# One attention tile per tick, two waves for the combination, and drains by name, in a hybrid decoder step

## The chip, the cores and the metric

The kernel runs on one core of a Trainium2 chip. The metric is the time of one execution on the device, in microseconds. The time before is the median of three runs. The engines are called by their short names: PE (TensorE, matrix products and transposes), DVE (VectorE), ACT (ScalarE), POOL (GpSimd) and SP (SyncE, which here issues every DMA, in the order of the program).

## The reference

One layer of a decoder trunk on a prompt of 1024 rows and a sample of 8 x 4 rows, D = 1024, all in float32:

```
h = RMSNorm(x);  [q|k|v|z|xBC|dt] = h @ w_in
attention: 12 heads of 64, RMS norm of q and k, ALiBi; three groups of 4 heads, (window, dilation) =
    (128,1), (512,4), (2048,16); query t reads t, t-d, ... t-window
    o_g = softmax(q k / 8 + bias) v;  alpha = softmax over g of lse_g;  att = concat(o_g * alpha_g)
SSD: causal conv (width 4) + SiLU on xBC; chunked scan, 16 heads of 64, state 128; D skip;
    * SiLU(z); RMSNorm
x = x + concat(att, ssd) @ w_out
u = causal conv (width 3) of RMSNorm(x) @ w_up;  x = x + (SiLU(gate) * up) @ w_down
```

The prompt and the sample are two batches with the same weights. The sample's attention also reads caches of keys and values, its SSD a state. New keys, values, states and convolution tails are outputs too.

## The kernel before

**Products.** Every projection is done three times, in a high and a low part: `hi x hi`, `hi x lo` and `lo x hi` (lines 1079 to 1081). Weights arrive by DMA (`w_load`), ACT makes the high part and DVE the low part (`w_split`, line 1069); three raw tiles and two high tiles take turns. A *chunk* is 128 output features for all 1056 rows, in three *units* of 352 columns; a unit of the xBC and z projections is 24 matmuls into one of three PSUM tiles `p_mm`, which DVE evicts (lines 1247 and 1561, scaled by the row factors `rb`).

**Stages.** First q, k and v of the three head groups (to about 332 us), with attention of groups 0 and 1 beside it. Then 12 xBC chunks, 8 z chunks, the out projection in two halves (attention, then SSD), and the feed-forward part.

**The side queues.** All other work is written as generators, held in named queues of a `Side` object. After each unit the program calls `tick`, which takes one step of each active generator; a generator that has just given PE work yields True, and is continued by `pre`, right after the next unit's matmuls and before that unit's eviction. So a generator's steps stand in the instruction streams between the units, and each engine runs its own stream in order. `add(name, gens, width, gap)` holds at most `width` active generators and opens one each `gap` ticks. `drain(names)` calls `pre` and `tick` with no unit between until the named queues are empty; `tick` steps all queues there.

**Around the change.** `att_gen` does one tile of 128 queries of one group: load of `qt` from the DRAM scratch `qscr`, transposes (line 663), scores into the one `p_sa` tile (682), bias and maximum by DVE (689), `Exp` by ACT (695), transposes (704), products with v (720), copies out (736). For group 2 a unit loads its rows by two strided DMAs (line 656), and takes a tick each for load, transposes, scores, exponential, transposes and products; its copies come with the next `pre`. `samp_gen` does the sample's attention of a group with POOL products and DVE sums, one cache tile `kt` a tick; `samp_comb` combines the groups for the sample (line 897 are its products). `comb_gen` waits for both and combines the prompt's groups: it makes the factors, transposes them (932), writes them to `fscr` and reads them back broadcast into `F` tiles, multiplies six tiles `c` = 0 to 5 by them (954, on POOL for even c and DVE for odd c) and stores them to `attscr`. Then the SSD opens (`ssd_gen`, first PE work at line 1298), and z chunk 4 may start only when the first SSD group is through and its gate is applied. `samp_ssd` is the sample's SSD; its first products are line 1475. `at_first` loads the combined tiles back and splits them into A0h/A0l and A1h/A1l, the moving tensors of the out projection.

**Memory.** SBUF tiles lie at addresses written out in `PLACES`; tiles whose lifetimes don't meet may share bytes, and a first write waits for the last reader of what lay there.

Of the kernel before, what the change touches and what calls it, by code (L numbers as in the profile page):

```python
# [10 lines left out]
F32 = mybir.dt.float32  # L11
# [8 lines left out]
S = 1024  # L20
# [96 lines left out]
def raw_ap(base, offset, dims):  # L117
# [28 lines left out]
    "P": ([128, 1024], F32, 2, 1, 2), "PT": ([128, 1024], F32, 1, 1, 2),  # L146
    "bias2": ([128, 4, 128], F32, 1, 3, 3.3), "qt2": ([128, 768], F32, 3, 3, 3.3), "qT2": ([128, 512], F32, 2, 3, 3.3),
    "P2": ([128, 512], F32, 2, 3, 3.3), "PT2": ([128, 512], F32, 1, 3, 3.3),
    "cs": ([128, 8, 3, 8], F32, 1, 3.5, 3.5), "mn": ([128, 8, 4], F32, 1, 3.5, 3.5), "ce": ([128, 8, 3, 4], F32, 1, 3.5, 3.5),
    "cwt": ([128, 8, 3, 4], F32, 1, 3.5, 3.5), "fT": ([12, S], F32, 1, 3.5, 3.5), "F": ([128, S], F32, 3, 3.5, 3.5),  # L150

    "sq_q": ([128, 1024], F32, 1, 1, 3), "so": ([128, 1024], F32, 1, 1, 3.3), "kt": ([128, 1024], F32, 3, 1, 3),
    "pr": ([128, 768], F32, 2, 1, 2), "bl": ([128, 144], F32, 1, 1, 3), "sc": ([128, 144], F32, 1, 1, 3),
    "ml0": ([128, 32], F32, 1, 1, 3.3), "ml1": ([128, 32], F32, 1, 1, 3.3), "ml2": ([128, 32], F32, 1, 1, 3.3),
    "snm": ([128, 128], F32, 1, 2, 3.3), "b16": ([128, 128], F32, 1, 2, 3.3), "bsel": ([128, 8], F32, 1, 2, 3.3),
    "smt": ([16, 136], F32, 1, 2, 3.3), "ats": ([128, 6, NS], F32, 1, 2, 3.3),

# [33 lines left out]
PLACES = {  # L191
    "ident": (77376,), "ones": (77984,), "neghalf": (77888,), "rb": (224992,), "rtok": (214272,), "ss": (155328,),
    "rr": (214848,), "cw": (112288,), "triu": (76832,), "par": (55744,), "pk": (69792,), "dt": (5248,),
    "acum": (70880,), "dend": (75488,), "cdec": (76064,), "acs": (56256,), "dtw": (70816,), "e128": (76000,),
    "cdecs": (76576,), "dsk": (65664,), "dsk2": (55680,), "rT": (214336,), "xsp": (33728,), "dtr": (32576,),
    "qg": (218432,), "xh": (163584,), "xl": (121536,), "xt": (56320, 20160, 35808, 24256), "jk": (16064,),
    "sx": (28352, 14016), "xr": (1152, 3200, 39904, 30400), "cst_in": (214848,), "cst_g": (33152,),
    "wqkl": (155392, 113344), "wqkh": (5824, 220480), "wvl": (201728, 41952), "wvh": (46304, 197376),
    "sb": (103072, 53280, 101024, 92832, 90784), "sq": (110240, 50656), "sm": (55424, 35776, 55392, 55648),
    "AU0": (78496,), "AU1": (20288,), "AU2": (43712,), "ac": (14144, 1152, 65696, 71392),  # L200
    "stt": (5024, 55456, 5152, 5088, 55328), "bias": (86688,), "qt": (94880, 97952, 38880, 1280),
# [5 lines left out]
    "ats": (8928,), "dt_x": (24064,), "dt_e": (20864,), "dt_s": (26688,), "dt_q": (21440,), "dt_p": (20288,),  # L207
    "na": (14016,), "acT": (4352,), "acTT": (24640, 22016), "wl": (10048, 117440, 159488), "wh": (155392, 113344),
    "XSa": (197376,), "XSb": (18368,), "zsm": (68768,), "ssq": (39360,), "BCa": (78496,), "BCb": (95392,),
    "BCs": (220256,), "xss": (60544,), "stc": (220768,), "ncv": (214848,), "st_in": (5824,), "ci0": (39360,),  # L210
    "ci1": (86688,), "acc": (91040, 107680), "zt": (52032, 220768, 14144, 43584), "Ab": (5824, 47808, 56320),
    "M": (61568, 103584), "xdt": (216160, 218208, 71392), "xdw": (35264, 73440), "cbm": (3200, 67744, 4224),
    "hn": (65696, 1152), "ho": (37312,), "sAb": (2176,), "sxdt": (61568,), "sxdw": (86816,), "scbm": (111904,),
# [5 lines left out]
    "facc": (219776, 197376, 30752), "nf": (9664, 39264, 9856, 9760, 39168, 213984, 9952, 9568), "tst": (214912,),  # L219
}  # L220
# [34 lines left out]
class Side:  # L255
# [7 lines left out]

    def add(self, name, gens, width=2, gap=1):
        ent = self.q.setdefault(name, [[], [], width, gap, 0])
        ent[0] += list(gens)
# [12 lines left out]

    def tick(self):  # L280
        waits = [g for _, g in self.early]
        for ent in list(self.q.values()):
            waiting, active, width, gap, left = ent
            ent[4] = max(left - 1, 0)
            if len(active) < width and waiting and not ent[4]:
                active.append(waiting.pop(0))
                ent[4] = gap
            for g in list(active):
                if not any(g is w for w in waits):
                    self.step(ent, g)  # L290
        self.q = {n: e for n, e in self.q.items() if e[0] or e[1]}

    def drain(self, names=None):
        while set(self.q) & set(names or self.q):
            self.pre()
            self.tick()


def body(tc, A):
# [338 lines left out]
    def bias_load(g, at):  # L638
# [3 lines left out]
        bias_t[g] = b  # L642

    def att_gen(g, i, at):
        qt = R("qt" + at)
        full = qscr[g].rearrange("t w c -> t (w c)")
        if g == 0:
            SP.dma_start(qt, full[i * 128:(i + 1) * 128, :])
            first = i == 0
        elif g == 1:  # L650
            r, blk = divmod(i, 2)
            SP.dma_start(qt, full[blk * 512 + r:(blk + 1) * 512:4, :])
            first = blk == 0
        else:
            for e in range(2):
                SP.dma_start(qt[e * 64:(e + 1) * 64], full[2 * i + e:S:16, :])
            first = True
# [85 lines left out]
    def att_chain(g, at):  # L743

        gens = [att_gen(g, i, at) for i in range(8)]
        return gens
# [9 lines left out]
    def samp_gen(g):  # L756
# [38 lines left out]
        for w, c in order:  # L795
# [40 lines left out]
            else:  # L836
# [5 lines left out]
                if c:  # L842
                    V.tensor_tensor(o, o, kt, op=ALU.add)
        done.add(("samp", g))
        yield
        SP.dma_start(oscr[g], o)
        yield

    def samp_comb():
# [7 lines left out]
        bsel = R("bsel")  # L857
        SP.dma_start(bsel, A["bsel"])
        yield
        ps = p_st()  # L860
# [26 lines left out]
        for g in range(3):  # L887
            o = R("so")
            SP.dma_start(o, oscr[g])
            yield  # L890
            V.tensor_tensor(o.rearrange("p (e d) -> p e d", d=64), o.rearrange("p (e d) -> p e d", d=64),
                            nm[:, 32 + g * 16:48 + g * 16, None].to_broadcast([128, 16, 64]), op=ALU.mult)
            yield
            for j in range(2):
                for t in range(4):
                    c = (2 * g + j) * NS + t * 8
                    T.matmul(ps[:, c:c + 8], lhsT=o[:, t * 256 + j * 128:t * 256 + (j + 1) * 128], rhs=bsel,
                             start=True, stop=True)
# [7 lines left out]
    def comb_gen():  # L906
# [40 lines left out]

        f_load(0)
        f_load(1)
        f_load(2)  # L950
        yield
        yield
        for c in range(6):
            (V if c % 2 else G).tensor_tensor(acs_[c], acs_[c], Fs.pop(c), op=ALU.mult)
            if c % 2:
                yield
                for x in (c - 1, c):
                    SP.dma_start(attscr[x, :, 0:S], acs_[x])
            if c < 3:
                f_load(c + 3)  # L960
        yield
# [181 lines left out]
    def group_end(g):  # L1143

        AUg[g] = R(f"AU{g}")
        if g < 2:
            bias_load(g, "")
            side.add("att", att_chain(g, ""), 4, 2)
        else:
            bias_load(2, "2")  # L1150
            side.add("att", att_chain(2, "2"), 4, 2)
        side.add("kvout", [kv_out(g)], 1)
# [429 lines left out]
    def at_low(c):  # L1582
        h, (raw, lo) = AT[c]
        (V if c % 3 else G).tensor_tensor(lo, raw, f32(h), op=ALU.subtract)

    def at_first():
        at_load(0)
        yield
        yield
# [8 lines left out]
    for f in range(8):  # L1598
        z_chunk(12 + f, f)
    at_load(1)  # L1600
    run_post(99)
# [299 lines left out]
```

## Time and profile before

| | |
|---|---|
| median of three runs | 1681.27 us (1681.21 to 1682.15) |
| profiled execution | 1682.31 us, of which the trace spans 1680.5 |
| PE busy | 1611.2 us |
| DVE, ACT, POOL busy | 1022.3, 618.5, 367.3 us |
| DMA | 159.9 MB, mean 95 GB/s |
| mean granted clock of PE | 0.985 |

The times of the trace count from the start of its span. A row of the timeline names an instruction's start, its duration, engine, line, operation, output and inputs, and in brackets how long the engine had been idle before it and what ended that. A granted clock of 1.00 is 2.4 GHz, one of 0.50 is 1.2 GHz.

### The profile page before, as it was taken

What the parts mean: (1) busy time and instruction counts of PE and PEld (TensorE: products, weight loads), DVE (VectorE), ACT (ScalarE), POOL (GpSimd) and SP (SyncE); (2) the same over time, 40 slices, a digit from 0 to 9 for tenths busy, and PEclk for the clock granted to TensorE, in tenths of its full rate; (3) what the DMA queues carried; (4) which work ended last, traced back from release to release, by engine and by line L of the source; (5) the groups of instructions that cost most, each with busy time, mean ns of one, the idle gap of its engine ahead of it and who ended that gap; (6) DMA issues with size and microseconds to landing.
All of it is one profiled execution on the core that took longest, in us unless ns stands there. A gap on an engine that the chain in (4) does not pass through costs nothing.

```text
span 1680.5 us, 26456 instructions
## 1 busy us (share of the span) xinstructions
PE 1611.2 (96%) x10543; PEld 1520.8 (90%) x10543; DVE 1022.3 (61%) x1714; ACT 618.5 (37%) x1144; POOL 367.3 (22%) x400
## 2 busy tenths in 40 slices
PE   7999989979979999799999999999999999999998
PEld 5787866879978888699999999999999999999998
DVE  5657648546557686874554665555655556555565
ACT  6534534436526876531223322131221312213121
POOL 3555345420023566420111100000000000000000
PEclk9999999989989999899999999999999999999999
DMA  7562365673392221574113102111021110211102
GB/s 216 160 185 66 115 214 165 208 177 113 86 248 98 67 95 57 170 210 119 43 43 101 52 26 68 48 39 52 26 67 49 38 52 26 65 51 38 52 1 105
DMA packets 174475, 159.91 MB, mean 95 GB/s; under 512 B 18851, under 2 KB 151355, under 8 KB 174352
## 3 DMA queue, kind: packets, MB, share of 16 engines
q1 hardware_dynamic: 174351, 158.22, 31.4%
q8 instruction: 83, 1.36, 0.3%
q14 instruction: 41, 0.33, 0.1%
HBM read 127.37 MB, written 34.42 MB: 96 GB/s over the span
## 4 chain that ended last, share of the span: by engine, by line
PE 72%; DVE 3%; DMA 2%; ACT 2%; issue 2%; POOL 1%; SPq 0%; DVEq 0%; POOLq 0%; ACTq 0%
PE p_up L1079 10%; PE p_up L1080 10%; PE p_up L1081 10%; PE p_mm L1079 6%; PE p_mm L1081 6%; PE p_mm L1080 6%; PE p_dn L1835 5%; PE p_dn L1836 5%; PE p_dn L1837 5%; DMA F<-fscr 1%; PE p_sa L1337 1%; DMA qt<-qscr 1%; PE p_sa L1330 1%; PE p_sa L1335 0%; POOL Ab L1322 0%
## 5 line engine op out<-in xcount | busy, mean ns | idle before, releaser
L1079 PE MATMUL p_up<-x2h,wh 128*128 128x352 f32 x1032 | 334.7, 324 | 0.0
L1080 PE MATMUL p_up<-x2l,wh 128*128 128x352 f32 x1032 | 333.4, 323 | 0.0
L1081 PE MATMUL p_up<-x2h,wl 128*128 128x352 f32 x1032 | 332.2, 322 | 0.0
L1745 DVE TENSOR_TENSOR fci<-p_up,rb 128x352 f32<-128x352 f32 x129 | 66.2, 513 | 238.1 <-PE p_up L1081 236.5
L1080 PEld LDWEIGHTS p_up<-x2l,wh 128*128 128x128 f32 x1032 | 194.3, 188 | 0.0
L1079 PEld LDWEIGHTS p_up<-x2h,wh 128*128 128x128 f32 x1032 | 193.8, 188 | 0.2
L1081 PEld LDWEIGHTS p_up<-x2h,wl 128*128 128x128 f32 x1032 | 193.8, 188 | 0.0
L1839 DVE TENSOR_TENSOR yacc<-yacc,p_dn 128x352 f32<-128x352 f32 x264 | 133.6, 519 | 75.2 <-PE p_dn L1837 75.2
L1835 PE MATMUL p_dn<-gp,dh 128*128 128x352 f32 x528 | 172.2, 326 | 0.0
L1836 PE MATMUL p_dn<-gp,dh 128*128 128x352 f32 x528 | 171.0, 324 | 0.0
L1837 PE MATMUL p_dn<-gp,dl 128*128 128x352 f32 x528 | 170.8, 323 | 0.0
L1081 PE MATMUL p_mm<-xh,wl 128*128 128x352 f32 x480 | 157.0, 327 | 10.0 <-DVE wl L1069 10.0
L1079 PE MATMUL p_mm<-xh,wh 128*128 128x352 f32 x480 | 162.6, 339 | 0.0
L1080 PE MATMUL p_mm<-xl,wh 128*128 128x352 f32 x480 | 156.3, 326 | 0.0
L1071 ACT CAST wh<-wl 128x512 fp32r<-128x512 f32 (+1 forms) x160 | 92.2, 606 | 112.1 <-PE p_up L1080 76.5
L1069 DVE TENSOR_TENSOR wl<-wl,wh 128x512 fp32r<-128x512 f32 (+1 forms) x160 | 126.0, 787 | 3.8 <-ACT wh L1071 3.7
L1763 DVE SCALAR_TENSOR_TENSOR facc<-fci,cw,facc 128x1072 f32<-128x1072 f32 x88 | 116.8, 1327 | 2.4 <-ACT facc L1755 2.4
L1782 ACT CAST gp<-facc 128x1024 fp32r<-128x1024 f32 (+1 forms) x44 | 25.7, 631 | 216.1 <-DVE facc L1778 216.1
L1081 PEld LDWEIGHTS p_mm<-xh,wl 128*128 128x128 f32 x480 | 91.6, 191 | 10.8 <-DVE wl L1069 10.8
L1835 PEld LDWEIGHTS p_dn<-gp,dh 128*128 128x128 f32 x528 | 99.2, 188 | 0.7 <-DVE yacc L1839 0.7
L1836 PEld LDWEIGHTS p_dn<-gp,dh 128*128 128x128 f32 x528 | 99.4, 188 | 0.0
L1837 PEld LDWEIGHTS p_dn<-gp,dl 128*128 128x128 f32 x528 | 99.1, 188 | 0.0
(390 smaller groups left out, 3436.9 us busy)
## 6 DMA issues: line engine op xcount, KB each, us to landing
wl<-in_w_up_dram SPq DMA_DIRECT2D x44, 512.0 KB
dl<-in_w_down_dram SPq DMA_DIRECT2D x22, 512.0 KB
kt<-in_cache_kv_dram SPq DMA_DIRECT2D x20, 512.0 KB
wl<-in_w_in_dram SPq DMA_DIRECT2D x20, 512.0 KB
Ab<-acscr SPq DMA_DIRECT2D x16, 512.0 KB
wqkl<-in_w_in_dram SPq DMA_DIRECT2D x24, 256.0 KB
qscr<-sb SPq DMA_DIRECT2D x24, 256.0 KB
qt<-qscr SPq DMA_DIRECT2D x16, 384.0 KB
```

What stands on the lines that cost most here:

```text
L1069: V.tensor_tensor(lo[:, c], raw[:, c], f32(hi[:, c]), op=ALU.subtract)
L1071: AC.copy(hi[:, c], raw[:, c])
L1079: T.matmul(ps[:, :CH], lhsT=hi[:, c], rhs=mh[:, c0:c0 + CH], start=k == 0, stop=False)
L1080: T.matmul(ps[:, :CH], lhsT=hi[:, c], rhs=ml_[:, c0:c0 + CH], start=False, stop=False)
L1081: T.matmul(ps[:, :CH], lhsT=lo[:, c], rhs=mh[:, c0:c0 + CH], start=False, stop=k == len(moving) - 1)
L1745: V.tensor_tensor(ci[:, 2 + c0:2 + c0 + w], ps[:, :w], r2t[:, c0:c0 + w], op=ALU.mult)
L1763: V.scalar_tensor_tensor(acc[:, :L], ci[:, i:i + L], cw_f[:, i, fu:fu + 1], acc[:, :L], op0=ALU.mult, op1=ALU.add)
L1782: AC.copy(hi, src)
L1835: T.matmul(ps[:, :CH], lhsT=hi[:, mc], rhs=GP[:, s2, c], start=x == 0, stop=False)
L1836: T.matmul(ps[:, :CH], lhsT=hi[:, mc], rhs=GP[:, s2 + 1, c], start=False, stop=False)
L1837: T.matmul(ps[:, :CH], lhsT=lo[:, mc], rhs=GP[:, s2, c], start=False, stop=x == len(fs) - 1)
L1839: V.tensor_tensor(yacc[:, m, c], yacc[:, m, c], ps[:, :CH], op=ALU.add)
```

## The change

- `add` has a `lead`: the number of ticks before the first generator opens. Group 2's attention now has width 8, gap 1 and lead 3 in place of width 4 and gap 2; its two first tiles are loaded in `group_end`, ahead of the bias; its `qt2` ring has six tiles in place of three.
- `samp_comb` loads the two stored results of the sample's groups at its start, into tiles of their own, keeps the third in SBUF without storing it, and multiplies the three without a tick for each load.
- `comb_gen` loads c = 0 to 2, waits three ticks, multiplies all three, then loads c = 3 to 5 and stores 0 to 2, waits three ticks, multiplies, and stores 3 to 5 two ticks later.
- `drain(names)` steps only the named queues, all queues each eighth time.
- `at_first` issues the loads of both halves of the combined tiles; the low part of c = 3 is made by DVE, not POOL.
- All addresses in `PLACES` are new, by a table not shown here. Of the tiles that the text speaks of, each 4224 bytes a partition, the four z buffers `zt` move from 52032, 220768, 14144, 43584 to 64384, 29408, 68608, 25184, and the three `A1h` from 14144, 52032, 43584 to 24928, 29152, 98176.

```diff
-    "bias2": ([128, 4, 128], F32, 1, 3, 3.3), "qt2": ([128, 768], F32, 3, 3, 3.3), "qT2": ([128, 512], F32, 2, 3, 3.3),
+    "bias2": ([128, 4, 128], F32, 1, 3, 3.3), "qt2": ([128, 768], F32, 6, 3, 3.3), "qT2": ([128, 512], F32, 2, 3, 3.3),
...
-    def add(self, name, gens, width=2, gap=1):
-        ent = self.q.setdefault(name, [[], [], width, gap, 0])
+    def add(self, name, gens, width=2, gap=1, lead=0):
+        ent = self.q.setdefault(name, [[], [], width, gap, lead])
...
-    def tick(self):
+    def tick(self, names=None):
         waits = [g for _, g in self.early]
-        for ent in list(self.q.values()):
+        for name, ent in list(self.q.items()):
+            if names is not None and name not in names:
+                continue
...
     def drain(self, names=None):
+        n = 0
         while set(self.q) & set(names or self.q):
+            n += 1
             self.pre()
-            self.tick()
+            self.tick(names if n % 8 else None)
...
+    def qt_strided(qt, i):
+        full = qscr[2].rearrange("t w c -> t (w c)")
+        for e in range(2):
+            SP.dma_start(qt[e * 64:(e + 1) * 64], full[2 * i + e:S:16, :])
+
+    ready = {}
+
     def att_gen(g, i, at):
-        qt = R("qt" + at)
+        qt = ready.pop((g, i)) if (g, i) in ready else R("qt" + at)
...
         else:
-            for e in range(2):
-                SP.dma_start(qt[e * 64:(e + 1) * 64], full[2 * i + e:S:16, :])
+            if i > 1:
+                qt_strided(qt, i)
             first = True
...
+        os_ = [R("sq_q"), R("so2"), last_o[0]]
+        for g in range(2):
+            SP.dma_start(os_[g], oscr[g])
...
         for g in range(3):
-            o = R("so")
-            SP.dma_start(o, oscr[g])
-            yield
+            o = os_[g]
...
-        f_load(0)
-        f_load(1)
-        f_load(2)
-        yield
-        yield
-        for c in range(6):
-            (V if c % 2 else G).tensor_tensor(acs_[c], acs_[c], Fs.pop(c), op=ALU.mult)
-            if c % 2:
+        for c in range(3):
+            f_load(c)
+        for half in range(2):
+            for _ in range(3):
                 yield
-                for x in (c - 1, c):
-                    SP.dma_start(attscr[x, :, 0:S], acs_[x])
-            if c < 3:
-                f_load(c + 3)
+            for c in range(3 * half, 3 * half + 3):
+                (V if c % 2 else G).tensor_tensor(acs_[c], acs_[c], Fs.pop(c), op=ALU.mult)
+            yield
+            if half:
+                yield
+            for c in range(3 * half, 3 * half + 3):
+                if c < 3:
+                    f_load(c + 3)
+                SP.dma_start(attscr[c, :, 0:S], acs_[c])
...
+            for i in range(2):
+                ready[2, i] = R("qt2")
+                qt_strided(ready[2, i], i)
             bias_load(2, "2")
-            side.add("att", att_chain(2, "2"), 4, 2)
+            side.add("att", att_chain(2, "2"), 8, 1, 3)
...
-        (V if c % 3 else G).tensor_tensor(lo, raw, f32(h), op=ALU.subtract)
+        (V if c else G).tensor_tensor(lo, raw, f32(h), op=ALU.subtract)
 
     def at_first():
         at_load(0)
+        at_load(1)
...
-    at_load(1)
     run_post(99)
     side.drain({"ssd", "yg", "conv_out", "at", "kvout"})
```

## Rows read from the trace of the kernel before

**Rows 1.** The page, part 1: PE's busy time, share and instructions.

```profile
PE 1611.2 (96%) x10543; PEld 1520.8 (90%) x10543; DVE 1022.3 (61%) x1714; ACT 618.5 (37%) x1144; POOL 367.3 (22%) x400
```

**Rows 2.** Waits of PE over the span: total us, times, longest.

```profile
PE p_st L663 <- DMA qt<-qscr: 14.4, 2, 9.7
PE p_mm L1081 <- DVE wl L1069: 10.0, 2, 6.0
...
PE p_st L1475 <- issue: 4.8, 1, 4.8
...
PE p_mm L1080 <- POOL A1l L1584: 2.0, 1, 2.0
```

**Rows 3.** Windows: busy us (instructions) of each engine, granted clock, DMA share, GB/s.

```profile
332.00:350.00 18.00, 8.26 (x52) 8.00 (x51) 2.25 (x4) 1.50 (x3) 2.34 (x3) 0.79 0.98 235
350.00:446.00 96.00, 95.87 (x676) 90.14 (x674) 58.41 (x149) 57.32 (x134) 13.32 (x24) 0.99 0.45 123
446.00:476.00 30.00, 30.00 (x190) 29.78 (x191) 18.92 (x35) 14.23 (x20) 2.65 (x7) 1.00 0.49 121
476.00:500.00 24.00, 13.98 (x75) 13.24 (x74) 11.15 (x11) 2.47 (x5) 5.78 (x6) 0.85 1.01 268
...
692.00:712.00 20.00, 15.20 (x94) 12.66 (x92) 17.77 (x12) 10.54 (x13) 11.58 (x5) 0.69 0.18 50
...
712.00:897.00 185.00, 185.00 (x1267) 178.64 (x1265) 104.31 (x171) 54.84 (x101) 31.77 (x17) 1.00 0.35 102
...
350.00:352.00 2.00, 2.00 (x9) 2.00 (x8) 0.00 (x0) 0.59 (x1) 1.31 (x2) 0.50 0.56 156
```

**Rows 4.** Timeline of SP's queue near 335 us; last, the chain's DMA row.

```profile
332.94 0.44 SPq L1230 DMA_DIRECT2D rb<-rscr  x1
...
335.23 0.66 SPq L759 DMA_DIRECT2D sq_q<-qs  x1
...
337.18 1.32 SPq L656 DMA_DIRECT2D qt<-qscr  x2
...
337.91 11.44 DMA qt<-qscr
```

**Rows 5.** Timelines of DVE and POOL, 338 to 358 us.

```profile
338.35 0.53 DVE L1247 TENSOR_TENSOR ci<-p_mm,rb 128x352 f32<-128x352 f32 x1 [9.74 <-DMA rb<-rscr]
...
347.91 2.34 POOL L832 TENSOR_TENSOR kt<-kt,sq_q 128x1024 f32<-128x1024 f32 x1 [15.63 <-DMA kt<-in_cache_kv_dram]
...
356.01 1.21 DVE L834 TENSOR_REDUCE sc<-kt 128x16 f32<-128x1024 f32 x1
357.13 0.28 DVE L689 CUSTOM_DVE_ANT_0 P<-p_sa,bias 128x128 f32<-128x128 f32 x1
```

**Rows 6.** Timeline of PE: the combination's transposes, and the SSD's first work.

```profile
465.27 1.03 PE L932 MATMUL p_st<-ident,ce 128*12 128x128 f32 x8
...
506.79 0.60 PE L1298 MATMUL p_st<-ident,XSa 128*128 128x128 f32 x4
```

**Rows 7.** Timelines of DVE and POOL at the combination's products.

```profile
480.12 1.23 DVE L954 TENSOR_TENSOR ac<-ac,F 128x1024 f32<-128x1024 f32 x1 [2.34 <-DMA ac<-attraw]
...
490.04 1.23 DVE L954 TENSOR_TENSOR ac<-ac,F 128x1024 f32<-128x1024 f32 x1 [6.81 <-DMA F<-fscr]
...
485.27 2.35 POOL L954 TENSOR_TENSOR ac<-ac,F 128x1024 f32<-128x1024 f32 x1 [2.19 <-DMA F<-fscr]
```

**Rows 8.** Timeline of ACT: first and last instruction for one SSD unit.

```profile
538.19 2.44 ACT L1314 ACTIVATE M<-Ab,acum 128x128 f32<-128x128 f32 x8
...
542.91 1.04 ACT L1316 ACTIVATE Ab<-Ab 128x1024 f32<-128x1024 f32 x1
```

**Rows 9.** Timelines of DVE and ACT at the end of the z chunks.

```profile
692.33 2.96 DVE L1584 TENSOR_TENSOR A0l<-A0l,A0h 128x1056 fp32r<-128x1056 f32 x1 [0.45 <-ACT A0h L1580]
...
696.70 1.25 DVE L1584 TENSOR_TENSOR A0l<-A0l,A0h 128x1056 fp32r<-128x1056 f32 x1
...
701.21 6.38 DVE L1584 TENSOR_TENSOR A1l<-A1l,A1h 128x1056 fp32r<-128x1056 f32 x2
...
700.24 1.08 ACT L1580 CAST A1h<-A1l 128x1056 fp32r<-128x1056 f32 x1 [0.76 <-POOL ssq L1549]
```

More of the change, by code (lines that the diff above doesn't have):

```diff
@@ L150 @@
     "cwt": ([128, 8, 3, 4], F32, 1, 3.5, 3.5), "fT": ([12, S], F32, 1, 3.5, 3.5), "F": ([128, S], F32, 3, 3.5, 3.5),
-    "sq_q": ([128, 1024], F32, 1, 1, 3), "so": ([128, 1024], F32, 1, 1, 3.3), "kt": ([128, 1024], F32, 3, 1, 3),
+    "sq_q": ([128, 1024], F32, 1, 1, 3.3), "so": ([128, 1024], F32, 1, 1, 3.3), "so2": ([128, 1024], F32, 1, 3, 3.3), "kt": ([128, 1024], F32, 3, 1, 3),
     "pr": ([128, 768], F32, 2, 1, 2), "bl": ([128, 144], F32, 1, 1, 3), "sc": ([128, 144], F32, 1, 1, 3),
@@ L155 @@
     "snm": ([128, 128], F32, 1, 2, 3.3), "b16": ([128, 128], F32, 1, 2, 3.3), "bsel": ([128, 8], F32, 1, 2, 3.3),
-    "smt": ([16, 136], F32, 1, 2, 3.3), "ats": ([128, 6, NS], F32, 1, 2, 3.3),
+    "smt": ([16, 136], F32, 1, 3, 3.3), "ats": ([128, 6, NS], F32, 1, 3, 3.3),
     "dt_x": ([128, 9, 16], F32, 1, 1, 1), "dt_e": ([128, 9, 16], F32, 1, 1, 1), "dt_s": ([128, 9, 16], F32, 1, 1, 1),
@@ L191 @@
 PLACES = {
[L192 to L201, printed above, removed]
[5 rows of a table removed]
@@ L207 @@
[L207 to L211, printed above, removed]
@@ L212 @@
-    "M": (61568, 103584), "xdt": (216160, 218208, 71392), "xdw": (35264, 73440), "cbm": (3200, 67744, 4224),
-    "hn": (65696, 1152), "ho": (37312,), "sAb": (2176,), "sxdt": (61568,), "sxdw": (86816,), "scbm": (111904,),
[5 rows of a table removed]
-    "facc": (219776, 197376, 30752), "nf": (9664, 39264, 9856, 9760, 39168, 213984, 9952, 9568), "tst": (214912,),
+    "ident": (19584,), "ones": (20096,), "neghalf": (20608,), "rb": (203776,), "rtok": (20704,), "ss": (20768,),
+    "rr": (19296,), "cw": (54624,), "triu": (220288,), "par": (159104,), "pk": (222336,), "dt": (223360,),
@@ new lines @@
+    "acum": (220800,), "dend": (221312,), "cdec": (221824,), "acs": (223936,), "dtw": (224000,), "e128": (224064,),
+    "cdecs": (224128,), "dsk": (54560,), "dsk2": (18752,), "rT": (55680,), "xsp": (41568,), "dtr": (159616,),
+    "qg": (127360,), "xh": (72832,), "xl": (169984,), "xt": (37472, 33376, 64384, 11904), "jk": (5760,),
+    "sx": (1152, 45664), "xr": (16000, 3712, 9856, 47712), "cst_in": (15168,), "cst_g": (3200,),
+    "wqkl": (203776, 56192), "wqkh": (25184, 211968), "wvl": (123008, 20832), "wvh": (68480, 224384),
@@ new lines @@
+    "sb": (43616, 110720, 134528, 49760, 106624), "sq": (120960, 51808), "sm": (160192, 160224, 160256, 160288),
+    "AU0": (139648,), "AU1": (11392,), "AU2": (3200,), "ac": (64384, 123264, 25184, 36608),
+    "stt": (53856, 53920, 53984, 54048, 54112), "bias": (45664,), "qt": (136576, 38496, 5248, 33376),
[5 rows of a table added]
+    "snm": (30304,), "b16": (30816,), "bsel": (31328,), "smt": (52320,), "ats": (52864,), "dt_x": (11392,),
+    "dt_e": (11968,), "dt_s": (12544,), "dt_q": (147840,), "dt_p": (148416,), "na": (148992,), "acT": (149056,),
@@ new lines @@
+    "acTT": (16704, 13120), "wl": (212096, 56192, 60288), "wh": (208000, 216192), "XSa": (131968,), "XSb": (148864,),
+    "zsm": (227968,), "ssq": (165760,), "BCa": (106624,), "BCb": (11392,), "BCs": (226432,), "xss": (226944,),
+    "stc": (31360,), "ncv": (130432,), "st_in": (148864,), "ci0": (68480,), "ci1": (47968,), "acc": (114816, 20832),
+    "zt": (64384, 29408, 68608, 25184), "Ab": (41824, 33632, 5248), "M": (37728, 119168),
+    "xdt": (3200, 45920, 124288), "xdw": (9344, 1152), "cbm": (224384, 225408, 123264), "hn": (126336, 52320),
@@ L220 @@
+    "ho": (128384,), "sAb": (224384,), "sxdt": (127616,), "sxdw": (9600,), "scbm": (16768,), "sBt": (17024,),
[5 rows of a table added]
+    "facc": (224608, 9344, 85088), "nf": (13664, 13760, 13856, 13952, 14048, 14144, 14240, 14336), "tst": (14432,),
 }
@@ L844, in samp_gen @@
         done.add(("samp", g))
+        if g == 2:
+            last_o.append(o)
         yield
-        SP.dma_start(oscr[g], o)
-        yield
+        if g < 2:
+            SP.dma_start(oscr[g], o)
+            yield
+    last_o = []
     def samp_comb():
@@ L946, in f_load @@
                 SP.dma_start(Fs[c][e2 * 64:(e2 + 1) * 64, :], raw_ap(fscr, (2 * c + e2) * S, [[0, 64], [1, S]]))
-        f_load(0)
-        f_load(1)
-        f_load(2)
-        yield
-        yield
-        for c in range(6):
-            (V if c % 2 else G).tensor_tensor(acs_[c], acs_[c], Fs.pop(c), op=ALU.mult)
-            if c % 2:
-                yield
-                for x in (c - 1, c):
-                    SP.dma_start(attscr[x, :, 0:S], acs_[x])
-            if c < 3:
-                f_load(c + 3)
+        for c in range(3):
+            f_load(c)
+        for half in range(2):
+            for _ in range(3):
+                yield
+            for c in range(3 * half, 3 * half + 3):
+                (V if c % 2 else G).tensor_tensor(acs_[c], acs_[c], Fs.pop(c), op=ALU.mult)
+            yield
+            if half:
+                yield
+            for c in range(3 * half, 3 * half + 3):
+                if c < 3:
+                    f_load(c + 3)
+                SP.dma_start(attscr[c, :, 0:S], acs_[c])
         yield
```

20 rows, old and new, of the table PLACES are left out of this document.

## The prediction, made before the changed kernel ran

> **What bounds the kernel now.** Read first the busy times of the engines: TensorE (PE) is busy 1611 of 1680.5 us [rows 1], so only what leaves PE idle, or running at the lower of its two clock levels, can be won back. Then the waits of PE [rows 2]: see that four causes hold most of what is left. Then windows laid around those waits [rows 3]: the stretch 446 to 476 has no hole and does 190 matmuls in 30 us, 0.158 us each, so a unit of 24 matmuls (one tick) costs 3.8 us. By that price, 332 to 350 does 52 matmuls, worth 8.2 us, and loses 9.8; 476 to 500 does 75, worth 11.9, and loses 12.1; and 692 to 712 runs at a granted clock of 0.69. From 712 on PE is full to the end, so nothing can be won there. Each hole is followed by slow work: in 350 to 352 the granted clock is 0.50 (the 1.2 GHz level) and 9 matmuls take what would hold 12.7, so 0.6 us more go there, and I allow 0.7 at the first hole and 0.9 at the second. The ceiling is thus 10.5 us at the first (**A**), 13 at the second (**B**), and a few at the end of the z chunks (**C**).
>
> **The change, part by part.** Ticks are counted from 0 at the first xBC unit.
>
> *Ticks.* Before, attention unit u opens at tick 2u and lives seven ticks, so unit 7 ends at 20; the combination opens at 21, transposes at its fourth tick (24, the row at 465.27) and ends at 30, so that the SSD opens at 31 (506.79) [rows 6]. Now unit u opens at tick 2+u and the last ends at 15. The sample combination loads its tiles together, not one a tick: its three products stand at ticks 13, 14 and 15 in place of 14, 16 and 18, and it ends at 16. The combination opens at 17 and has four waiting ticks more, 13 in place of 9: the SSD opens at 31 again. From there on the order of ticks is as before. No matmul is added or removed; only holes can move the end.
>
> *A, first rows loaded ahead.* Before, SP issues rb, bias, weights, sq_q, the first kt and then the first qt, from 337.18 on; it lands at 337.91 + 11.44 = 349.35 [rows 4], and PE waits 9.7 us for it (14.4 in all, the rest in an earlier stage) [rows 2]. Now four half loads stand right behind rb, and the first transpose comes after four units, at 332 + 4 x 3.8 = 347. Issued by about 337 (they wait for the last stores of their scratch), they land near 342: this wait is gone. What is late next is the sample's first product: sq_q and kt are now queued behind 0.77 MB more. They let POOL start at 347.91 before [rows 5]; four more SP issues of 0.65 us and 0.77 MB at 235 GB/s [rows 3] (3.3 us, in part overlapping) put this at 349 to 351.5. VectorE (DVE) runs in order: its reduction of that tile (1.2 us) is put in at tick 2, ahead of the evictions and of the first score reduction (1 us), and two more reductions follow POOL's 2.4 us products. So the score tile, of which there is one, is free some 3 x 2.4 + 1.2 + 1.5 = 10 us after POOL starts, at 359 to 361.5, while PE, unhindered, wants it for unit 1 after tick 5, at 332 + 6 x 3.8 + 2.5 = 357. That gives back 2 to 4.5 us and about 0.7 for the clock. I take A = 7; bounds 2 (everything behind waits for the same bytes) and 10.5.
>
> The Trainium skill (DMA: Bandwidth & Descriptors, "Two DMAs through the same engine are not ordered") says that a transfer reading what an earlier one wrote must wait for that one's completion. It speaks against loads right behind the stores of their scratch: SP would stand there and hold all issues behind it. No row here shows this place; by the rule alone the sample's loads would be some 2 us later, and A 5 us.
>
> *B, two waves.* Before, the six products were put in at one or two ticks after their loads. DVE stood 2.3 us for the second and 6.8 us for the fourth [rows 7], the splits of the next weights stood behind it, and PE waited 10.0 us for them [rows 2], at 24 us of 268 GB/s [rows 3]. The loads of c=3 to 5 also waited in SP for the product that frees their F tile. Now the loads of wave one have two units and more, about 12.5 us from the transposes' end, before DVE meets its product; the second tile landed 480.12 - 466.1 = 14 us after it before, with a fourth ac and F mixed in, so DVE stands 0 to 1.5 us. Wave two has 3.5 MB; at 268 GB/s that is 13 us, after F's last load has waited for POOL's second product (about 19 us after the transposes). Its F lands near 31 us, DVE's last product is due at about 29 to 31. DVE stands 1 to 2 us, and two units lie between it and the splits that PE needs: no hole. I take 12 of 13; bounds 6 (the last load as late again as half of before) and 13.
>
> *D, dense attention.* Each tick between 7 and 10 now holds a whole unit's work. In 350 to 446 PE does 676 matmuls; 434 are the 18 units' (68 us), the rest, 28 us, is attention and sample combination, so ticks 2 to 16 last about 15 x 3.8 + 28 = 85 us. ScalarE (ACT) with 57.3 and DVE with 58.4 us [rows 3] of work for all 18 fit into that even whole, but in the dense ticks both come to some 85 to 90%, and table loads bunch in one of three. A later unit's rows are put in one tick ahead, as before. Nearest row for a PE wait of this kind is below 2 us (POOL, DVE releasers in [rows 2]): I take -1.5, bounds 0 and -5.
>
> *C, drains and the last products.* At the end of the z chunks the drain takes three ticks. Now it leaves out the sample SSD queue: its matmuls (behind which PE waited 4.8 us [rows 2]) come behind the first out-projection unit. But the first projection matmuls also need A0l of c=0 and 1, and DVE's runs from 692.33, unchanged; PE starts at most 0.6 us sooner. Then the last subtraction of A1: DVE took 6.4 us for two while POOL worked on a third, against 1.25 for one alone [rows 9]. With c=3 on DVE and no POOL beside it, three cost 3.8. Against it, A1h of c=3 and 4 now lie on the fourth z buffer and must wait for POOL's sum as c=5 did at 700.24 [rows 9]. The sequence 700.2 + 1.0 (cast) + 3.8 ends near 705; before the last wait ended at 707.6. Of these 2.6 us and the 0.6 above, about 2 go back as the sample work moved into later ticks. I take +1; bounds -2 and +4. The sample state ends three ticks later, still one unit before the second projection wants its norm; were that cover gone, about 5 us.
>
> The Trainium skill (GPSIMD Engine Reference, "Specifications") says POOL shares its SBUF interfaces with DVE instructions of two SBUF inputs. The trace agrees: 3.2 us each beside POOL, 1.25 alone [rows 9].
>
> The other layout of addresses has, by the byte ranges, no further reuse whose last user is later than the next tile's first write would be. Where tick 0 stands nothing changes: the drain before it is already empty, PE passes it without a wait.
>
> **Sum.** A 7 + B 12 + C 1 - D 1.5 = 18.5 us. The profiled execution took 1682.31 us (its span is 1680.5), so it becomes 1663.8; the median of the runs, 1681.27, lies 1.04 lower: 1663.
>
> **Rivals.** *The first hole stays fed by the same bytes.* 332 to 350 moves 235 GB/s at a share of 0.98, and the change only reorders; PE then waits at the first score matmul, with DVE behind the sample. A 2, B 12, C 0, D -4: 10 us, 1671. For it speaks the full DMA, against it that PE needs only two small tiles by then. *Only the holes move.* 24 us of DMA at a share of 1.01 remain in the combination, and wave two waits on its last F; B 2, A 2, D -4: 1681, no change. Against it: four ticks, 15 us, are added just there. *Slower, by one mechanism:* the longer combination opens the SSD later. z chunk 4 (tick 48) may not start before the first SSD group is through, which happens only a tick before; each tick too late is one without projection matmuls, and costs about the 5.7 us that ACT needs for one SSD unit (538.19 to 543.95) [rows 8]. It decides from the first tick by which attention or sample ends later than my 16; four ticks late are 23 us, against 18.5 won: 1686. By the count of ticks this is a balance of zero, without reserve.
>
> **How the numbers follow.** Chances: forecast 0.67, first hole stays 0.20, holes only move 0.06, slower 0.07. 0.2%, 3.4 us, is about what the runs can tell from no change. Faster takes the first two, 0.87; same 0.06; slower 0.07. The terms' bounds add up to 1654 and 1680; the ends are unlikely together, so the range is 1655 to 1674, which leaves out the last two cases and a little at each side.
>
> **What would show it.** Right: no PE wait on qt after 300 us; a shorter one of the score matmul at tick 5, released by DVE; no PE wait for wl near the combination; the SSD's first transposes near 488, not 506.8; the psi matmuls behind the first projection matmuls. Wrong: PE waits for ACT in the dense ticks above 5 us in all, idle ticks before z chunk 4, a DMA that keeps DVE standing over 8 us at the products of either wave, or holes in the part after 712.

## The result, and the profile after

The changed kernel takes 1665.09 us (median of four runs, 1662.15 to 1669.93), against 1681.71 for the kernel before on that chip: a ratio of 0.989 (0.985 to 0.993). The forecast was 1663, its range 1655 to 1674. The profiled execution is the slowest of the four, 1669.93 with a span of 1668.1, so its parts explain 12.4 us of span, some 4 less than the medians show.

The waits of PE from 300 to 720 us (total, times, longest) answer to [rows 2]:

```profile
PE p_sa L694 <- DVE stt L701: 9.3, 1, 9.3
PE p_mm L1098 <- ACT A0h L1602: 4.9, 1, 4.9
PE p_sa L1357 <- POOL Ab L1344: 3.2, 4, 1.7
PE p_mm L1099 <- POOL A0l L1606: 2.2, 1, 2.2
```

See what is gone: qt (9.7 us at this place before), wl (10.0) and the wait before psi (4.8). And see what is new at the top: a score matmul, L694, waits 9.3 us for DVE's score reduction, L701. The windows answer to [rows 3]:

```profile
332.00:350.00 18.00, 18.00 (x117) 17.98 (x116) 2.84 (x6) 3.72 (x6) 0.00 (x0) 1.00 0.89 231
...
332.00:368.00 36.00, 26.73 (x177) 26.11 (x175) 13.19 (x27) 5.10 (x10) 9.26 (x7) 0.93 0.89 234
368.00:434.00 66.00, 66.00 (x478) 61.34 (x477) 39.44 (x116) 45.61 (x121) 5.56 (x14) 0.96 0.36 94
434.00:495.00 61.00, 61.00 (x382) 60.76 (x382) 44.03 (x60) 22.07 (x30) 10.06 (x18) 1.00 0.69 214
674.00:700.00 26.00, 17.57 (x109) 15.54 (x108) 19.83 (x27) 15.85 (x18) 7.50 (x5) 0.74 0.32 107
```

PE now runs through 332 to 350, where it lost 9.8 us, but 332 to 368 still loses 9.3: the hole has moved by one attention unit. The stretch of the combination, 434 to 495, is full and at full clock; that hole is gone. The end of the z chunks has its hole still.

SP's queue and the chains on DVE and POOL answer to [rows 4, 5]. SP:

```profile
330.69 3.12 SPq L636 DMA_DIRECT2D qscr<-sb  x3
333.86 0.53 SPq L1252 DMA_DIRECT2D rb<-rscr  x1
337.35 2.42 SPq L652 DMA_DIRECT2D qt<-qscr  x4
...
340.92 0.64 SPq L771 DMA_DIRECT2D sq_q<-qs  x1
...
342.25 1.18 SPq L790 DMA_DIRECT2D kt<-in_cache_kv_dram  x2
```

POOL, then DVE:

```profile
354.07 4.73 POOL L844 TENSOR_TENSOR kt<-kt,sq_q 128x1024 f32<-128x1024 f32 x2 [22.22 <-DMA kt<-in_cache_kv_dram]
```

```profile
356.50 1.22 DVE L846 TENSOR_REDUCE sc<-kt 128x16 f32<-128x1024 f32 x1 [11.29 <-POOL kt L844]
...
363.58 1.21 DVE L846 TENSOR_REDUCE sc<-kt 128x16 f32<-128x1024 f32 x1
...
366.08 0.29 DVE L701 CUSTOM_DVE_ANT_0 P<-p_sa,bias 128x128 f32<-128x128 f32 x1
```

Read this as one chain. SP stands from 334.4 to 337.35 in front of the four row loads, and so the sample's query, which went out at 335.23 before, goes out at 340.92. POOL's product starts at 354.07 in place of 347.91. DVE stands 11.3 us for it, and unit 0's score reduction comes behind all three sample reductions, at 366.08 (357.13 before). Unit 1 has no second score tile, so PE stands.

Two rows of PE answer to [rows 6], one of DVE to [rows 7]:

```profile
451.27 0.93 PE L950 MATMUL p_st<-ident,ce 128*12 128x128 f32 x7
...
494.81 0.38 PE L1320 MATMUL p_st<-ident,XSa 128*128 128x128 f32 x2
```

```profile
479.93 2.90 DVE L972 TENSOR_TENSOR ac<-ac,F 128x1024 f32<-128x1024 f32 x1
```

Between the combination's transposes and the SSD's first ones lie 43.5 us in place of 41.5, but full of work. DVE met its products without standing: this row has no idle time before it, nor have the rows of its other two. In again DVE stands 0.4 and 2.1 us at two of the three.

A ledger by stage, from PE's first matmul of each (us; the last three columns are runs of the next section; the last z matmul is here the last one of `hi x hi`, counted at its start):

```
                                 before  after  again  idle3  late3
first xBC matmul at               331.9  332.8  334.2  333.1  333.6
to the SSD's first transposes     174.9  162.0  159.9  171.9  162.7
from there to the last z matmul   179.1  179.3  179.3  164.2  163.5
to the first up-projection        221.6  220.4  221.8  219.4  219.2
to the end                        773.1  773.6  773.7  773.7  773.3
```

Nearly all that the change won lies in the second line: 12.9 us in this execution, 15.0 in another of the same kernel ("again"). Before, 332 to 350 and 446 to 507 held the two holes; the second stretch, 61 us, held 298 matmuls, worth 47.1 at 0.158 us each, so it lost 13.9; 434 to 495 holds 382 now, worth 60.4, and loses 0.6. The second hole was thus worth 13.3, and the first between -0.4 and 1.7.

### The profile page after: what moved, and what is told of

It is laid out like the page before. It is cut to its first block, busy times and chain, and to the rows that moved or that the text cites. A ratio compares the mean times of both kernels' runs of the same rounds, so it can differ in the third digit from the quotient of the medians.

```text
span 1668.1 us, 26440 instructions
## 1 busy us (share of the span) xinstructions
PE 1610.2 (97%) x10543; PEld 1521.3 (91%) x10543; DVE 1013.3 (61%) x1715; ACT 614.3 (37%) x1140; POOL 359.5 (22%) x399
## 4 chain that ended last, share of the span: by engine, by line
PE 73%; issue 2%; DMA 2%; POOL 2%; DVE 2%; ACT 1%; SPq 0%; POOLq 0%; DVEq 0%
PE p_up L1100 10%; PE p_up L1098 10%; PE p_up L1099 10%; PE p_mm L1098 7%; PE p_mm L1099 6%; PE p_mm L1100 6%; PE p_dn L1857 5%; PE p_dn L1858 5%; PE p_dn L1859 5%; DMA kt<-in_cache_kv_dram 1%; POOL Ab L1344 1%; PE p_sa L1359 1%; PE p_sa L1352 1%; PE p_sa L1357 0%; PE p_tr L1838 0%
## 5 line engine op out<-in xcount | busy, mean ns | idle before, releaser
L1780 POOL COPY nf<-fci 128x18 f32<-128x18 f32 x44 | 9.7, 220 | 396.6 <-DVE fci L1769 396.6
```

## The experiments

Each was timed beside the kernel before, on the same chip. Ratios are to the kernel before, whose median lay between 1681.71 and 1685.55 us. Four ran first.

**again**: the changed kernel unchanged.

> The changed kernel itself, beside the others on their chip. Theory: what differs from run to run is the score matmul's stop at tick 5 behind the sample's first cache tile, so its runs lie between 1660 and 1670 us and the median near 1664. Rival: the spread comes from TensorE's clock in the long part after 700 us; then a profile with the same stop of some 9 us can have a span of 1660.

1668.39 us, 0.9907 (0.989 to 0.992). The score wait was 7.9 us. This ratio is the yardstick for what follows. Its runs, 1665.98 to 1671.86, lie higher than expected. The theory on the spread is not borne out: this profile waits 1.4 us less for the score than that of the result and is 0.8 us longer. Nor does the rival's long part differ: from the first up-projection matmul on, all profiles here take 773.1 to 773.8 us. The stage ahead of the first xBC matmul, which nothing here touches, differs by 6 us between profiles, and the way from the last z matmul to the up-projection by 4.5.

**one_wave**: the old loop of the combination, everything else new.

```
-        for c in range(3):
-            f_load(c)
-        for half in range(2):
...
+        f_load(0)
+        f_load(1)
+        f_load(2)
+        yield
+        yield
+        for c in range(6):
```

> The changed kernel with the combination loop of the kernel before (two idle ticks, then a product at each tick or two, each product's store and load in between). Theory: the two waves are worth the whole second hole, so PE waits about 10 us for low weight parts again and the time is 10 to 13 us above the changed kernel's, near 1676. Rival: the first hole's order had filled the DMA queue and so caused the second; then the old loop costs 3 us at most here. The combination ends four ticks sooner in this kernel, at 26, so a gain from an SSD that opens at tick 27 could take some of it back: then the product waits show and the time does not.

1682.65 us, 0.999 (0.998 to 1.000). The old loop costs some 14 us, nearly the whole change; all else that is new, the addresses among it, is worth little beside it. The wait for the next weights is back:

```profile
PE p_mm L1099 <- DVE wl L1087: 7.2, 2, 5.1
```

The SSD opened at 488.7, earlier than in any other kernel here, and nothing was won by it. By the 28th projection unit, just ahead of that opening, one_wave is 10.3 us behind again; by the 59th it is 14.6. So about 10 us are the hole itself, and the rest falls in the stage of the SSD, whose opening the old loop moves as well.

**idle3**: three empty ticks at the end of the sample combination.

```
+        for _ in range(3):
+            yield
```

> The changed kernel with three empty ticks behind the sample's combination, so that the prompt's combination opens at tick 20 and the SSD at 34. Theory: the ticks are in balance without reserve, z chunk 4 has to wait, and three ticks without projection matmuls cost about 5.7 us each: 17 us, 1681. Rival: the SSD's units are only moved, PE has its work in any order, and three ticks cost 0 to 3 us.

1663.82 us, 0.988 (0.987 to 0.989). The theory fell, and with it the reason that the slower rival gave: opening three ticks late won some 4 us. (The two intervals meet at 0.989; from the first xBC matmul on, the profile is 5.5 us shorter than again's.) The ledger shows where: the SSD opens 12.0 us later, counted from the first xBC matmul, but the way from there to the last z matmul is 15.1 shorter. By the number of projection units (24 matmuls each) done since the first xBC unit, the first transposes of the SSD's units come after

```
again  32 34 36 38 40 41 42 43 44 45 46 47 49 50 51 52
idle3  35 37 39 40 41 42 43 44 45 46 47 48 49 50 51 52
```

Up to the tick at which the second SSD group is put in, one SSD unit starts every second tick, and from then on one each tick. A later opening mostly skips starts at the slow pace, and the last units begin at the same places. Of the three late ticks one is left: ahead of z chunk 4 (after 48 units) one tick passes without projection matmuls, and PE stands 1.1 us in it. The gain itself is holes: from 500 to 550 PE stood 6.9 us in again and 0.9 in idle3, where other parts of SSD units fall together. That window of again, then of idle3:

```profile
500.00:550.00 50.00, 43.07 (x314) 39.02 (x314) 36.42 (x49) 39.02 (x69) 18.77 (x15) 1.00 0.23 67
500.00:550.00 50.00, 49.08 (x357) 45.85 (x356) 39.48 (x54) 38.59 (x76) 20.25 (x15) 1.00 0.32 99
```

Again's waits from 500 to 652 us:

```profile
PE p_sa L1357 <- POOL Ab L1344: 3.9, 4, 1.7
PE p_st L1419 <- ACT ho L1421: 2.0, 1, 2.0
PE p_sa L1352 <- DVE M L1343: 1.7, 1, 1.7
```

**drain_all**: the drains step all queues again.

```
-            self.tick(names if n % 8 else None)
+            self.tick()
```

> The changed kernel with drains that step all queues, as before. Theory: at the one drain with work left the first projection matmuls wait for the split of the first tile anyway, so leaving the sample's queue out is worth about 1 us, and less than 2. Rival: the 4.8 us that PE stood at the sample's first SSD products before are won in full; then this kernel is 4 to 6 us slower.

1667.92 us, 0.9909 (0.990 to 0.992): no difference from again. The wait before psi is back, at no cost:

```profile
PE p_st L1497 <- issue: 4.8, 1, 4.8
```

Of the next four, samp_first and no_reduce asked why the first hole stayed.

**samp_first**: the four row loads go behind the sample's query and first key.

```
-            for i in range(2):
-                ready[2, i] = R("qt2")
-                qt_strided(ready[2, i], i)
+            def qt_first():
+                for i in range(2):
+                    ready[2, i] = R("qt2")
+                    qt_strided(ready[2, i], i)
+                yield
+            side.add("qt", [qt_first()], 1)
```

> The first-row loads of units 0 and 1 (four transfers) are put in behind the sample's query and first key loads instead of ahead of them, nothing else changes. Theory (the score matmul of unit 1 waits because the four loads ahead of the sample's make SyncE stand about 3 us for the scratch's stores and cost issues, so the sample's first product starts 6 us later than before the change): the product starts near 348 to 350 us, the score wait at tick 5 falls from 8 to 9 us to 4 us or less, a transpose waits 0 to 3 us for its rows, and the time lies 4 to 8 us under the change as it is. Rival (the same bytes feed the same hole in any order): the wait moves to the first rows, the sum of both stays 8 us or more, and the time is within 2 us of the change as it is.

1670.47 us, 0.9909 (0.989 to 0.993). POOL's product did start 4.5 us sooner than in the profile of the result, at 349.53 (counted from the first xBC matmul, 3.2 sooner than there and 1.8 sooner than in again), and the score wait shrank, but the rows were late instead. The sample's first tile was issued 6.4 us sooner, at 335.87, and then took 13.7 us to POOL's start in place of 11.8. Its waits from 332 to 440:

```profile
PE p_st L675 <- DMA qt<-qscr: 4.5, 2, 3.9
PE p_sa L694 <- DVE stt L701: 3.4, 1, 3.4
```

The sum is the 7.9 of again: here the rival held.

**no_reduce**: DVE's three reductions of the third sample group are left out, so that group's scores are not computed.

```
-                V.tensor_reduce(sc[:, c * 16:(c + 1) * 16], ...)
+                if g < 2:
+                    V.tensor_reduce(sc[:, c * 16:(c + 1) * 16], ...)
```

> VectorE's three score reductions of the third sample group are left out (the sample attention's scores of that group are then not computed), all its loads and GpSimd's products stay. Theory (VectorE runs in order and stands for GpSimd's products in front of unit 1's score reduction): the score wait at tick 5 is gone or below 2 us, and the time lies 7 to 10 us under the change as it is. Rival (something else, a transfer or ScalarE, holds unit 1 at that place as well): the wait stays above 4 us with another releaser, and under 4 us are gained.

1666.90 us, 0.989 (0.987 to 0.991): 3 us or less are won, and the score matmul still waits 5.3, for DVE as before. The rows of DVE and POOL show why:

```profile
353.31 3.34 DVE L1285 SCALAR_TENSOR_TENSOR acc<-ci,cw,acc 128x1080 f32<-128x1080 f32 x1
356.58 2.38 DVE L814 TENSOR_TENSOR sc<-sc,bl 128x48 f32<-128x48 f32 x1
...
359.23 2.38 DVE L817 TENSOR_TENSOR sc<-sc,ml 128x48 f32<-128x48 f32 x1
```

```profile
353.12 5.77 POOL L844 TENSOR_TENSOR kt<-kt,sq_q 128x1024 f32<-128x1024 f32 x2 [21.20 <-DMA kt<-in_cache_kv_dram]
...
359.18 2.33 POOL L844 TENSOR_TENSOR kt<-kt,sq_q 128x1024 f32<-128x1024 f32 x1
```

Two instructions over 48 columns, 0.21 and 0.24 us in after, took 2.38 each and ended with POOL's products. So even without its own waits DVE is held at POOL's pace, and POOL's by the data; unit 0's score reduction, behind them in DVE's order, came at 362.14.

**at_before**: the queue of the out-projection's operands is stepped ahead of the sample SSD's.

```
-    side.add("ssds", [samp_ssd()], 1)
...
     side.add("at", [when({("ssd", 0), ("ssd", 1), "conv"}, at_first)], 1)
+    side.add("ssds", [samp_ssd()], 1)
```

> The queue that makes the operands of the out-projection is stepped ahead of the sample SSD's queue in each tick, so that ScalarE's first casts (A0h) come ahead of the sample's exponentials. Theory (the 4.9 us wait for A0h after the last z chunk is ScalarE's order of work, with the projection's other operands close behind): that wait falls to 2 us or less, 1 to 3 us are gained, the rest of it going to the wait for GpSimd's A0l. Rival (the norm's sum, not the order on ScalarE, sets the start): the wait stays above 4 us and the time within 1 us.

1670.31 us, 0.9912 (0.989 to 0.993). The first projection matmul came 0.8 us after the start of the last z matmul (5.5 in again), but PE then waited 4.1 us for A0h in three pieces. The way from there to the up-projection was 219.0 us (222.7 in combo, which has the same order), against 218.2 to 221.8 in the kernels that have the old order: no gain that shows, in the times or there. The rival held.

**combo**: samp_first, at_before and idle3 together.

> samp_first, at_before and the three empty ticks behind the sample combination together. If the three places are independent, the gains add: 4 to 8 for the score wait, 1 to 3 for the casts, 4 to 5 for the empty ticks, so 9 to 16 us under the change as it is, near 1654 us. If the empty ticks' gain comes from the same place as another's, 5 to 8 us, near 1661.

1666.16 us, 0.988 (0.986 to 0.990): idle3's ratio. The gains did not add, since two of the three had none.

Of the last three kernels, two moved the point at which DVE meets the sample. That moves the sample's later loads in SP's queue too: the rows of unit 2 are issued at 349.93 in late3, at 360.50 in after. The third went on from idle3.

**late3**: the third sample group waits three ticks between its first loads and its first product. **late2** has a 2 there.

```
         ahead(1)
         yield
+        if g == 2:
+            for _ in range(3):
+                yield
         for w, c in order:
```

> The third sample group waits three ticks between its first loads and its first product, and everything behind it (its combination, the combination of the groups, the SSD) comes three ticks later, as with the three empty ticks behind the sample combination. Theory (the score matmul of unit 1 waits since VectorE meets the sample's products before their data is there; GpSimd's product starts with the data at 350 to 354 us either way): VectorE puts unit 0's and unit 1's score reductions ahead of the sample's, the score wait of 8 to 9 us falls below 2 us, and the time is 6 to 9 us under the run with three empty ticks, 10 to 13 under the change as it is, near 0.981 of the kernel before. Rival (the full DMA feeds the stretch 332 to 368 at the same pace whatever comes first, and a later unit or the next weights wait instead): the same 8 us show up as waits for transfers or for VectorE within 370 to 400, and the time is that of the three empty ticks, 0.988.

1654.44 us (1653.42 to 1659.82), 0.983 (0.981 to 0.985): the fastest kernel here; its interval lies clear of again's and of idle3's. From 332 to 440 PE waited 0.6 us for rows and 0.2 for ACT. DVE, in order:

```profile
356.76 0.28 DVE L701 CUSTOM_DVE_ANT_0 P<-p_sa,bias 128x128 f32<-128x128 f32 x1
...
362.04 1.21 DVE L849 TENSOR_REDUCE sc<-kt 128x16 f32<-128x1024 f32 x1
363.17 0.28 DVE L701 CUSTOM_DVE_ANT_0 P<-p_sa,bias 128x128 f32<-128x128 f32 x1
```

Units 0 and 1 have their scores before and beside the sample's. The whole gain over idle3, whose SSD opens at the same tick, is made here: by the eighth projection unit late3 is 9.7 us ahead, counted from the first xBC matmul, and by the 59th 9.9. The window of late3, to set beside the one of after above:

```profile
332.00:368.00 36.00, 35.43 (x240) 34.38 (x240) 17.90 (x43) 13.02 (x31) 7.88 (x11) 1.00 0.91 241
```

Nearly the same share of DMA, 240 matmuls in place of 177, and no fall of the clock. So the rival that had looked right after samp_first falls: the number of bytes did not bound this stretch. That the order on DVE did is read from its rows; the sample's later loads moved with it, and no run parts the two.

**late2**, with two ticks:

> The same with two ticks. Theory: the first reduction of the sample is then put in at the tick in which its data lands, so the score wait is 0 to 4 us, and the time lies between the change as it is and the run with three ticks, near 0.984 of the kernel before. Rival: 0.988 to 0.991, no difference from the change as it is beyond what empty ticks give.

1668.34 us, 0.9905 (0.989 to 0.992). The waits at the first hole:

```profile
PE p_st L675 <- DMA qt<-qscr: 4.2, 1, 4.2
...
PE p_sa L694 <- DVE stt L701: 0.9, 1, 0.9
```

The score wait fell to 0.9 us, as the theory wanted, but PE waited 4.2 us for the rows of unit 2, and SP shows the kv store ahead of their loads, issued at 345.97, taking 4.1 (2.7 in late3). So the order of the loads counts as well: here the hole came back in part as a wait for rows. The SSD's first units came after 34, 36, 38 and 40, the pattern of again rather than of idle3, and 500 to 530 lost 4.2 us. Against idle3 this kernel is 2.9 us ahead by the 32nd projection unit and 4.1 behind by the 40th. The time expected was wrong by 11 us and fell where the rival had it: the number of empty ticks also sets how SSD units meet the second group's opening.

**idle6**: idle3 with six.

> Six empty ticks behind the sample combination in place of three, so that the SSD opens at tick 37. Theory from the three empty ticks (the SSD's units are put in every second tick until the second group opens and every tick from then on, so a start three ticks later catches up; its last unit stood at the same projection unit in both): six ticks are more than the catching up can take, about two ticks come late, z chunk 4 stands for them at some 5.7 us each, and the time is 5 to 12 us above the run with three, 0.991 to 0.995 of the kernel before. Rival (the SSD's opening has still more reserve, or ticks without projection cost nothing): within 2 us of the run with three, 0.988.

1670.27 us, 0.992 (0.990 to 0.993), as expected, but only in part for the reason given. Three ticks passed without projection between 587.0 and 606.65, where idle3 has one; PE stood 4.5 us of that time and did the SSD's own matmuls in the rest. As large a loss is another wait, with a clock of 0.83 from 530 to 540 behind it:

```profile
PE p_st L1324 <- ACT ho L1423: 4.8, 1, 4.8
```

## Why the prediction was right, step by step

The direction and the mechanism of B were right, and the time fell into the range; of the two large terms one was right and one far too large. That the median came within 2 us of the forecast is in part luck, as the sum below shows.

- **B, two waves, +12.** Right: 13 by the windows, 10 to 14 by one_wave. DVE stood 0 us at its products in after and 0.4 and 2.1 in again, about as forecast, though POOL waited 6.2 and 4.5 us for the loads of its first two. The four extra units were the cover, as argued; no run has the waves without them. The count of ticks held: the SSD's first unit comes after 32 projection units, before and after. It opened at 494.81, not near 488, mostly since A did not come.
- **A, rows ahead, +7.** The failed step: "That gives back 2 to 4.5 us and about 0.7 for the clock." The wait for qt went as forecast, and its successor was named rightly, the score matmul at tick 5, wanted at 357.88 for a forecast 357. But it stood 9.3 us (7.9 in again), and some 2.6 more went to the lower clock level behind it (a mean of 0.96 over the 66 us from 368 on), where 0.7 had been allowed. A is nothing to 2. Two more sizes were off. The product began at 354.07, not at 349 to 351.5, since SP stood 2.9 us for the scratch's stores besides issuing four loads in 2.4. Behind the sample's loads, in samp_first, the same four were issued without that stand. And from there to the free score tile it took 12.9 us, not 10, partly because DVE's instructions stretch beside POOL (the split at 359.98 took 2.00 us, 0.68 elsewhere). The stand of SP is what the Trainium skill (DMA: Bandwidth & Descriptors, "Two DMAs through the same engine are not ordered") led one to fear; the trace agrees, at 2.9 us. The rule's price for A, 5, was also too kind.
- **The rival "fed by the same bytes", 1671.** It gave A rightly as 2, but its cause fell: late3 moves as many bytes in that stretch, at 241 GB/s against 234, without the hole.
- **D, dense attention, -1.5.** It cost nothing: from 368 to 434 PE is busy 66.00 of 66 us in after. ACT and DVE at some 60 to 70% of that stretch were enough.
- **C, drains and last products, +1.** Between +1.2 and -0.2 by the ledger. The drains are worth 0 (drain_all). PE starts its projection 5.5 us after the start of the last z matmul in place of 8.9, and has lost that by the 17th matmul of the projection (14.6 us, against 13.7 before).
- **The slower rival, 5.7 us per late tick.** Its balance was wrong: idle3 is three ticks late and faster. One tick without projection comes with three late ticks, three with six, and PE stands 1.1 and 4.5 us in them, not 5.7 each, for it has the SSD's own work there.
- **The sum.** With B 13, A 0 to 2, C 0 and D 0 it is 13 to 15 where 18.5 were forecast. From the first xBC matmul on, the two profiled executions of the changed kernel are 13.3 and 14.0 us shorter than that of before; the stage ahead of it, untouched by the change, took 0.9 and 2.3 longer in them (its end moved between 331.4 and 337.4 over all profiles here). The medians fell by 16.6 and 16.3; the 2 to 3 us between are not placed, and by the placed parts alone the time would be 1666 to 1668: inside the range, but 3 to 5 us above the forecast.

What stays open: that idle3's gain comes from how SSD units fall together is read from the starts and the waits; nothing was run to change that alone. Nor was the order on DVE changed with SP's order kept.

## What to carry to other kernels

Where an engine runs in order, moving a load earlier is half a change: ask which instruction then meets its data first, and what is queued behind it. Here the point at which DVE met the sample's product decided most, and not the number of bytes: three empty ticks there took the hole away, which the reordering of the loads had only moved. With two, a row load came late in its place, so both queues have to be looked at. And give a chain of products its distance from its loads, as the two waves did, before making anything else faster.

## What the runs showed of the hardware

DVE's small instructions with two SBUF operands did not merely slow down beside POOL: 48 columns took 2.38 us against 0.21, and ended at 358.96 and 361.61, when POOL's products ended at 358.89 and 361.51. The score reductions, which read PSUM and SBUF, kept their 0.28 us beside a product (356.49 in late2, POOL busy from 355.31 to 357.69), and the sample's sums over one operand their 1.2. With longer instructions it is the same: the combination's product at 479.93 ended at 482.83, 1.1 us after POOL's (479.34 to 481.74), which is about its length alone (1.21). It goes the other way too: the two products of POOL at 353.12 took 5.77 us, 1.1 more than twice 2.33, and a DVE instruction with two SBUF operands ended among them, at 356.65. So the price is the rest of the other engine's instruction, not a factor, and it is dearest for the smallest instructions. The Trainium skill (SBUF — State Buffer, "Who interferes with whom") says that the port pair which the two engines share is an exclusive lock, that a DVE instruction with two SBUF inputs contends with a GpSimd instruction that reads SBUF, and that one with at most one SBUF input, outside the 2-port modes, does not; the trace agrees: 2.38 us in place of 0.21 for the one kind, 0.28 and 1.2 as alone for the other. Not every instruction with one SBUF operand goes free here: the `tensor_scalar` over 4 columns behind the score reductions took 0.84 us at 367.04 in after and ended at 367.88, when POOL's product ended at 367.86; in late3, at 357.72 with POOL idle, it took 0.17. The prediction had read [rows 9] as a slowdown.
